# The four weight sums of each pair, made by adding DMAs in place of VectorE sums

## The chip, the cores and the metric

The kernel runs on one NeuronCore of a Trainium2 chip. The metric is device time in microseconds (us), the median of three executions. Engines in the views: PE is TensorE (PEld its weight loads), DVE is VectorE, ACT is ScalarE, POOL is GpSimd, SP is SyncE, which here only issues DMAs. A "q" after an engine's name (SPq, ACTq) is its instruction queue when it issues a DMA.

## What is computed

A decoder block over 1024 tokens of width 1024, in fp32: a pooling mixer and a sliding-window attention, merged by sigmoid gates, then a squared-ReLU MLP. The change touches two of its matrix products, the gates and the first MLP matrix:

```python
proj = jnp.einsum('bsd,de->bse', h, w_in[l]) + b_in[l]
u_pool, q, k, v, gates = jnp.split(proj, IN_SPLITS, axis=-1)      # gates: 2048 columns
...
g = jax.nn.sigmoid(gates.astype(jnp.float32)).astype(x.dtype)
...
ff = jnp.einsum('bsf,fd->bsd',
                jnp.square(jax.nn.relu(jnp.einsum('bsd,df->bsf', h2, w_up[l]))), w_down[l])
```

## The kernel before

Every fp32 operand of a matmul is split into a rounded part `hi` and a rest `lo`: `split` (L99 to L104) has ACT copy the source into `hi` (L101) and DVE subtract (L104). A block of 128x512 results then costs three matmul passes (`PASSES`) for each 128 of the contraction.

Gates and up both go through the class `Pairs`. It takes output rows of 128 in pairs and computes each pair by a 2x2 block scheme with seven products where the plain one has eight. Row 2p of the weights lies in a raw tile `r0` of 128x1024: its left half is A11, its right half A12. Row 2p+1 lies in `r1`: A21 and A22. There are 8 pairs for the gates and 16 for up. The seven products use these weight operands, by number:

- 1: A11; 2: A12; 4: A22 (no sum needed)
- 5: S1 = A21 + A22 (L492, into a tile `ws` of the pool `ga`)
- 6: S2 = S1 - A11 (L495); 7: S3 = A11 - A21 (L502); 3: S4 = A12 - S2 (L499)

`load` (L481) loads a raw tile from DRAM, `operand(p, i)` makes the sum and the split, `mm` (L515, matmuls at L519) runs the 12 matmuls of a product, `m1` and `m2` run products 1 and 2, and `rest` runs 6, 7, 5, 4 and 3 in this order, with DVE adding the results out of PSUM between them (L540 to L560). The other side of each product (`T1` to `T4`) are sums of blocks of the activations: `build_gate` makes them for the gates (from L722), `build_second` for up (from L1061). `gate_close0`, `gate_close1` and `up_close0`, `up_close1` apply sigmoid or relu and square, and store.

Gates: a first part runs products 1 and 2 of all pairs (`first`, `second`) in an order written out by hand for PE, DVE, ACT and SP; within it stand the operands 6 and 7 of pair 0 and `build_gate` for the blocks kt = 1, 2, 3. The loop after it runs `rest` for pairs 0 to 7. Up: a part with an order written out by hand for PE, DVE and ACT runs products 1 and 2 of pairs 0 to 6, builds the T tiles and makes pair 0's operands; then `rest(0)` and a loop over pairs 1 to 15, in which pairs from 7 on run their products 1 and 2 too. Outside the parts written by hand, a planner decides when the program is built in which order each engine takes its instructions: by when its own clock says that they are ready, and by program order among those. On the chip the order of each engine is fixed; an instruction whose data is late holds up all behind it on its engine.

Buffers: raw tiles come from `st` (3 slots) and, for the odd row of later pairs, from `g` (17 slots). Split operands 5, 6, 7 go to `ga` (6 slots) for the gates and `x1` (4 slots) for up, the others to `wh` (6 slots). Before the change POOL issues no DMA; the loads are issued by SP, stores by SP and ACT.

Of the kernel before, what the change touches and what calls it, by code (L numbers as in the profile page):

```python
# [8 lines left out]
F32 = mybir.dt.float32  # L9
# [41 lines left out]
def block_kernel(ctx: ExitStack, tc, xt, x, consts, vecs, sinks, b_qkv, g_post, g_mlp, g_mlp_post,  # L51
# [96 lines left out]
    vec = cp.tile([P, V_N], F32, name="vec")  # L148
# [68 lines left out]
    for k in range(NK):  # L217
        xs = at("s4", 4, [S])
        ws = stage([768]) if k else ws_first
        if k < 2:  # L220
            if k == 0:
                nc.sync.dma_start(vec, vecs)
            for a, b in ((0, 256), (256, 512)) if k == 0 else ((0, 512),):
                nc.sync.dma_start(xs[:, a:b], xt[k][:, a:b])
            if k:
                nc.sync.dma_start(ws, w_qkv[k])
            else:
                nc.sync.dma_start(ws[:, 512:], w_qkv[k][:, 512:])
            later.append((k, xs))
        else:  # L230
            nc.sync.dma_start(xs, xt[k])
            nc.sync.dma_start(ws, w_qkv[k])
            if k == 2:
                for i, t in later:
                    nc.sync.dma_start(t[:, 512:], xt[i][:, 512:])
# [32 lines left out]
    dve.tensor_scalar(nsnk, snk, -1.0, None, ALU.mult)  # L268

# [199 lines left out]

    OPERAND = {1: "B11", 2: "B21", 3: "B22", 4: "T4", 5: "T1", 6: "T2", 7: "T3"}  # L470

    class Pairs:


        def __init__(self, src, big, result, close_first, close0, close1):
            self.src, self.big, self.result = src, big, result
            self.close_first, self.close0, self.close1 = close_first, close0, close1
            self.X = {n: [None] * 4 for n in OPERAND.values()}
            self.raw, self.w, self.sums, self.f0, self.b1 = {}, {}, {}, {}, {}
# [6 lines left out]
        def operand(self, p, i):  # L486

            r0, r1_ = self.raw[2 * p], self.raw.get(2 * p + 1)
            if i in (5, 6, 3):
                if p not in self.sums:  # L490
                    self.sums[p] = ga_.tile([P, 2, 4, P], F32, tag="ga", name=nm("ws"))
                    dve.tensor_tensor(self.sums[p][:, 0], r1_[:, :4], r1_[:, 4:], ALU.add)  # L492
                src, s2 = self.sums[p][:, 0], self.sums[p][:, 1]
                if i == 6:
                    dve.tensor_tensor(s2, src, r0[:, :4], ALU.subtract)  # L495
                    src = s2
                elif i == 3:
                    src = r0[:, 4:]
                    dve.tensor_tensor(src, src, s2, ALU.subtract)  # L499
            elif i == 7:  # L500
                src = r0[:, :4]
                dve.tensor_tensor(src, r0[:, :4], r1_[:, :4], ALU.subtract)  # L502
            else:
                src = r0[:, :4] if i == 1 else r0[:, 4:] if i == 2 else r1_[:, 4:]
            t = self.big([2, 4, P]) if i in (5, 6, 7) and p else wslot([2, 4, P])
            split(t[:, 0], t[:, 1], src)
            self.w[p, i] = t
# [25 lines left out]
        def rest(self, p, f1, b6, b7, b5, done=(), then=None, b4=None):  # L533
# [4 lines left out]
            if 6 not in done:  # L538
                self.mm(b6, p, 6)
            dve.tensor_tensor(u2, u2, b6, ALU.add)  # L540
# [3 lines left out]
            if 7 not in done:  # L544
                self.mm(b7, p, 7)
# [151 lines left out]
    def gate_close(m, f):  # L697
        act.activation(f, f, AF.Sigmoid, bias=vec[:, V_BG + m:V_BG + m + 1])
        nc.scalar.dma_start(z_dram[m], f)
# [5 lines left out]
    def gate_close1(m, f):  # L705
        dve.tensor_tensor(f, f, rb, ALU.mult)
        gate_close(m, f)
# [14 lines left out]
    def build_gate(kt, place):  # L722

        ab = raw_x.pop(kt)
        act.activation(ab[0], ab[0], AF.Identity, scale=vec[:, V_G + kt:V_G + kt + 1])
        gb = vec[:, V_G + 4 + kt:V_G + 5 + kt]
        a0, a1, b0, b1 = (t[:, th * 512:(th + 1) * 512] for t in ab for th in range(2))
# [128 lines left out]
    with tc.manual_schedule(engines={mybir.EngineType.PE, mybir.EngineType.DVE, mybir.EngineType.Activation,  # L856
# [7 lines left out]
        for p in range(NG0):  # L864
# [39 lines left out]
    for p in range(8):  # L904
# [6 lines left out]
        for i in (6, 7, 5, 4, 3) if p else (5, 4, 3):  # L911
            gt.operand(p, i)
# [148 lines left out]
    def build_second(kt, b12, b22):  # L1061
# [4 lines left out]
        dve.tensor_tensor(r11, b12, r11, ALU.subtract)  # L1066
        dve.tensor_tensor(t2, b22, r11, ALU.subtract)
        dve.tensor_tensor(t3, b22, t3, ALU.subtract)
        dve.tensor_tensor(r21, r21, t2, ALU.subtract)
# [41 lines left out]
    def up_close1(m, f):  # L1111
        act.activation(f, f, AF.Relu)
# [66 lines left out]
    with tc.manual_schedule(engines={mybir.EngineType.PE, mybir.EngineType.DVE, mybir.EngineType.Activation}):  # L1179
# [25 lines left out]
        up.m2(2)  # L1205
        up.operand(0, 6)
        up.operand(0, 7)
# [338 lines left out]
```

## Time and profile before

| | us |
|---|---|
| median of 3 runs (lowest, highest) | 1115.41 (1114.57, 1115.86) |
| span of the profiled execution | 1112.6 |
| median less span | 2.8 |
| PE busy in the span | 1103.8 |
| DVE busy | 813.4 |
| ACT busy | 529.2 |
| POOL busy | 53.9 |
| gates: products 1 and 2 | 161.3 to 204.8 |
| gates: `rest`, pairs 0 to 7 | 204.8 to 313.9 |
| up: products 1 and 2 among transposes, pair 0 | about 480 to 547 |
| up: `rest`, pairs 1 to 15 | about 547 to 822 |
| second MLP matrix and end | 822 to 1112.6 |

The span runs from the first to the last instruction of the profiled execution; the time of a run has besides it what lies around the program. In the rows of the trace a group is given by line, engine, operation and "out<-in" with the shapes, then how often (x) and its busy time; in the timeline each row starts with its start and its length in us, and brackets tell how long the engine was idle before and what ended the wait.

### The profile page before, as it was taken

To read this page: it belongs to the slowest core of one execution; us is meant where nothing else is said; L and a number is where in the kernel's file an instruction comes from. 1 tells how busy PE (TensorE), PEld (TensorE's weight loads), DVE (VectorE), ACT (ScalarE), POOL (GpSimd) and SP (SyncE) were. 2 spreads that over 40 slices of the span, in tenths; PEclk is the share of its full clock that TensorE was granted. 3 is DMA by queue.
4 is the path that set the end of the run, shared out by engine and by line. 5 is a ranking of instruction groups with operands and counts; after the bars stand their busy time and mean duration, and the time that the engine had idled before them with its cause. 6 is when DMAs were issued, how large, how long until landed. Compare 5 with 4: busy or idle time off the path is not lost.

```text
span 1112.6 us, 13941 instructions
## 1 busy us (share of the span) xinstructions
PE 1103.8 (99%) x5162; PEld 916.6 (82%) x5162; DVE 813.4 (73%) x1217; ACT 529.2 (48%) x912; POOL 53.9 (5%) x104
## 2 busy tenths in 40 slices
PE   9999999999999999999999999999999999999997
PEld 8888888888888888888888888888888888888886
DVE  6578877898859966768978876766548945447797
ACT  7566656444323333636644544354444435344342
POOL 0334100000000500000000000000000000000000
PEclk9999999999999999999999999999999999999999
DMA  9615566366973543322356553434697766332652
GB/s 345 162 39 165 154 189 231 126 215 206 275 264 107 196 158 119 133 95 96 113 210 220 195 190 123 189 123 168 230 374 275 236 191 191 100 104 64 225 190 92
DMA packets 84435, 196.89 MB, mean 177 GB/s; under 512 B 7952, under 2 KB 20880, under 8 KB 84368
## 3 DMA queue, kind: packets, MB, share of 16 engines
q1 hardware_dynamic: 78608, 176.22, 47.1%
q10 hardware_dynamic: 5760, 19.79, 4.7%
q8 instruction: 40, 0.66, 0.2%
q14 instruction: 27, 0.22, 0.1%
HBM read 140.41 MB, written 55.58 MB: 176 GB/s over the span
## 4 chain that ended last, share of the span: by engine, by line
PE 96%; DVE 2%; ACT 1%; issue 0%; DVEq 0%; ACTq 0%
PE mm L519 25%; PE at L519 15%; PE at L1334 15%; PE mm L1334 12%; PE mm L1017 7%; PE mm L456 5%; PE mm L609 3%; PE mm L458 3%; PE mm L192 2%; PE mm L183 2%; PE sc L183 2%; PE sc L429 1%; PE sc L360 1%; PE at L1017 1%; PE at L1046 1%; PE sc L403 1%
## 5 line engine op out<-in xcount | busy, mean ns | idle before, releaser
L1334 PE MATMUL at<-ar,wh 128*128 128x512 f32 x696 | 158.7, 389 | 0.0
L1334 PEld LDWEIGHTS at<-ar,wh 128*128 128x128 f32 x696 | 130.6, 188 | 27.1
L1334 PE MATMUL mm<-ar,wh 128*128 128x512 f32 x576 | 131.0, 389 | 0.0
L1334 PEld LDWEIGHTS mm<-ar,wh 128*128 128x128 f32 x576 | 108.1, 188 | 22.5
L104 DVE TENSOR_TENSOR wh<-raw,wh 128x1024 fp32r<-128x1024 f32 x51 | 62.4, 1223 | 86.2 <-ACT wh L101 86.1
L101 ACT CAST wh<-raw 128x1024 fp32r<-128x1024 f32 x51 | 53.7, 1053 | 132.8 <-PE at L1334 53.8
L101 ACT CAST wh<-st 128x512 fp32r<-128x512 f32 (+1 forms) x104 | 65.6, 642 | 92.0 <-DVE st L499 25.8
L104 DVE TENSOR_TENSOR wh<-st,wh 128x512 fp32r<-128x512 f32 (+1 forms) x105 | 78.4, 756 | 37.3 <-ACT wh L101 34.7
L519 PE MATMUL mm<-gr,wh 128*128 128x512 f32 x333 | 79.3, 390 | 0.0
L519 PEld LDWEIGHTS mm<-gr,wh 128*128 128x128 f32 x333 | 62.2, 188 | 12.8
L519 PE MATMUL mm<-T,wx 128*128 128x512 f32 x288 | 67.4, 389 | 0.0
L519 PEld LDWEIGHTS mm<-T,wx 128*128 128x128 f32 x288 | 54.1, 188 | 11.2
L519 PE MATMUL at<-T,wx 128*128 128x512 f32 x252 | 58.9, 389 | 0.0
L519 PEld LDWEIGHTS at<-T,wx 128*128 128x128 f32 x252 | 47.3, 188 | 9.8
L519 PE MATMUL mm<-x,wh 128*128 128x512 f32 x240 | 55.2, 389 | 0.0
L519 PEld LDWEIGHTS mm<-x,wh 128*128 128x128 f32 x240 | 45.0, 188 | 9.4
L609 PE MATMUL mm<-x,wh 128*128 128x512 f32 x192 | 47.7, 395 | 0.0
L104 DVE TENSOR_TENSOR ar<-B,ar 128x1024 fp32r<-128x1024 f32 x37 | 45.1, 1220 | 2.3 <-ACT ar L101 2.0
L609 PEld LDWEIGHTS mm<-x,wh 128*128 128x128 f32 x192 | 35.2, 188 | 7.5 <-DVE qt L104 0.2
L101 ACT CAST ar<-B 128x1024 fp32r<-128x1024 f32 x37 | 38.9, 1051 | 4.7 <-DVE B L1305 2.8
L519 PE MATMUL at<-gr,wh 128*128 128x512 f32 x150 | 36.6, 390 | 0.0
L519 PE MATMUL mm<-T,wh 128*128 128x512 f32 x147 | 36.1, 389 | 0.0
(391 smaller groups left out, 2164.1 us busy)
## 6 DMA issues: line engine op xcount, KB each, us to landing
raw<-f_dram SPq DMA_DIRECT2D x53, 512.0 KB, 3.6
f_dram<-g SPq DMA_DIRECT2D x28, 512.0 KB, 3.3
st<-in_w_up_dram SPq DMA_DIRECT2D x24, 512.0 KB, 3.6
B<-in_w_dn_dram SPq DMA_DIRECT2D x24, 512.0 KB, 7.4
st<-in_w_g_dram SPq DMA_DIRECT2D x18, 512.0 KB, 4.2
f_dram<-g ACTq DMA_DIRECT2D x17, 512.0 KB, 3.1
g<-spill_dram SPq DMA_DIRECT2D x16, 512.0 KB, 5.0
raw<-in_w_dn_dram SPq DMA_DIRECT2D x16, 512.0 KB, 4.6
```

Source lines behind the costliest of these rows:

```text
L101: act.copy(hi, src)
L104: eng.tensor_tensor(lo, src, f32(hi), ALU.subtract)
L183: pe.matmul(bq, xs_[k][n // 4][:, xh, n % 4 * P:(n % 4 + 1) * P], wq[k][:, h, :], start=k == 0 and j == 0, stop=k == NK - 1 and j == 2)
L192: pe.matmul(bkv_of(n), xs_[k][n // 4][:, xh, n % 4 * P:(n % 4 + 1) * P], wkv[k // 2][:, h, k % 2, :], start=k == 0 and j == 0 and not (joi ...
L360: pe.matmul(sb[:, kv, i, :nk], qt[r, qx, m * P:(m + 1) * P], kx[r, k0:k0 + nk], start=j == 0, stop=j == 2)
L403: pe.transpose(bs[:, kv, m], s8[:, kv, m], ident)
L456: pe.matmul(bs[th], whi[:, k, :], rhs(k, hl, th), start=k == 0 and hl == 0, stop=False)
L458: pe.matmul(bs[th], wlo[:, k, :], rhs(k, 0, th), start=False, stop=k == nk - 1)
L519: pe.matmul(b, w[:, wh, kt, :], xo[kt][:, xh, :], start=not after and kt == 0 and j == 0, stop=kt == 3 and j == 2, skip_group_check=after)
L609: pe.matmul(b, (whi, wlo)[h][:, k, :], xr(k, xh, th), start=j == 0, stop=j == len(mms) - 1)
L1017: pe.matmul(obs[n][dj], l, wos[k][whl][:, dj * 512:(dj + 1) * 512], start=k == 0 and hl == 0 and whl == 0, stop=k == NK - 1 and hl == 1)
L1334: pe.matmul(bs[t], fo[fh][:, k2, t * P:(t + 1) * P], wo_[wh][:, k2, :], start=not after and s2 == 0 and k2 == 0 and j == 0, stop=(s2, k2) ...
```

## The change

The four sums of a pair are no longer made by DVE. GpSimd issues for each a DMA that adds a half row (128x512 fp32, 256 KB) from the weights in DRAM onto the half of a raw tile in SBUF. So that every sum is an addition, the second block row is taken with its sign turned: operand 7 is A11 + A21 (onto A11 in `r0`), operand 6 adds A22 to that, operand 3 adds A12 to that, and operand 5 is A21 + A22 (onto A21 in `r1`). Operands 7, 6 and 3 are so made one after the other in the same 128x512 of SBUF, each after the split of the one before has read it. The order in `rest` and in the calls of `operand` becomes 7, 6, 5, 4, 3. The turned signs are taken up by the T tiles (an addition for a subtraction, with the negated gain `neg_g` in `build_gate`), by one subtraction in `rest`, and by scale=-1 in `gate_close1` and `up_close1`. The tile `ws` goes away.

```diff
+    neg_g = vec[:, V_N:]
...
+    dve.tensor_scalar(neg_g, vec[:, V_G + 4:V_G + 8], -1.0, None, ALU.mult)
...
+    ADDEND = {7: (1, 0), 6: (1, 1), 3: (0, 1), 5: (1, 1)}
...
         def operand(self, p, i):
             r0, r1_ = self.raw[2 * p], self.raw.get(2 * p + 1)
-            if i in (5, 6, 3):
-                if p not in self.sums:
-                    self.sums[p] = ga_.tile([P, 2, 4, P], F32, tag="ga", name=nm("ws"))
-                    dve.tensor_tensor(self.sums[p][:, 0], r1_[:, :4], r1_[:, 4:], ALU.add)
-                src, s2 = self.sums[p][:, 0], self.sums[p][:, 1]
-                if i == 6:
-                    dve.tensor_tensor(s2, src, r0[:, :4], ALU.subtract)
-                    src = s2
-                elif i == 3:
-                    src = r0[:, 4:]
-                    dve.tensor_tensor(src, src, s2, ALU.subtract)
-            elif i == 7:
-                src = r0[:, :4]
-                dve.tensor_tensor(src, r0[:, :4], r1_[:, :4], ALU.subtract)
-            else:
-                src = r0[:, :4] if i == 1 else r0[:, 4:] if i == 2 else r1_[:, 4:]
+            src = r0[:, 4:] if i == 2 else r1_[:, 4:] if i == 4 else r1_[:, :4] if i == 5 else r0[:, :4]
+            if i in ADDEND:
+                row, half = ADDEND[i]
+                nc.gpsimd.dma_start(src, self.src[2 * p + row][:, 4 * half:4 * half + 4], accum_op=ALU.add)
             t = self.big([2, 4, P]) if i in (5, 6, 7) and p else wslot([2, 4, P])
             split(t[:, 0], t[:, 1], src)
...
         def rest(self, p, f1, b6, b7, b5, done=(), then=None, b4=None):
-            if 6 not in done:
-                self.mm(b6, p, 6)
-            dve.tensor_tensor(u2, u2, b6, ALU.add)
+            if 7 not in done:
+                self.mm(b7, p, 7)
             if p in self.b1:
                 self.f0[p] = f0
                 self.m2(p)
-            if 7 not in done:
-                self.mm(b7, p, 7)
+            if 6 not in done:
+                self.mm(b6, p, 6)
+            dve.tensor_tensor(u2, u2, b6, ALU.subtract)
...
-        gate_close(m, f)
+        gate_close(m, f, -1.0)
...
-        dve.tensor_tensor(a0, a1, a0, ALU.subtract)
+        dve.tensor_tensor(a0, a0, a1, ALU.subtract)
         dve.scalar_tensor_tensor(a1, b1, gb, a1, ALU.mult, ALU.subtract)
-        dve.scalar_tensor_tensor(b1, b1, gb, a0, ALU.mult, ALU.subtract)
-        dve.scalar_tensor_tensor(b0, b0, gb, b1, ALU.mult, ALU.subtract)
+        dve.scalar_tensor_tensor(b1, b1, gb, a0, ALU.mult, ALU.add)
+        dve.scalar_tensor_tensor(b0, b0, ngb, b1, ALU.mult, ALU.add)
...
             if p == 6:
-                gt.operand(0, 7)
+                gt.operand(0, 6)
...
             if p == 5:
-                gt.operand(0, 6)
+                gt.operand(0, 7)
...
-        for i in (6, 7, 5, 4, 3) if p else (5, 4, 3):
+        for i in (7, 6, 5, 4, 3) if p else (5, 4, 3):
...
-        act.activation(f, f, AF.Relu)
+        act.activation(f, f, AF.Relu, scale=-1.0)
...
+        up.operand(0, 7)
         up.operand(0, 6)
-        up.operand(0, 7)
...
-        for i in (6, 7, 5, 4, 3) if first else (1, 6, 2, 7, 5, 4, 3):
+        for i in (7, 6, 5, 4, 3) if first else (1, 7, 2, 6, 5, 4, 3):
```

`build_second` changes its four DVE sums in the same way.

More of the change, by code (lines that the diff above doesn't have):

```diff
@@ L147, in block_kernel @@
     cst = cp.tile([P, C_N], F32, name="cst")
-    vec = cp.tile([P, V_N], F32, name="vec")
+    vec = cp.tile([P, V_N + 4], F32, name="vec")
+    neg_g = vec[:, V_N:]
     snk = cp.tile([P, NH], F32, name="snk")
@@ L221, in block_kernel @@
             if k == 0:
-                nc.sync.dma_start(vec, vecs)
+                nc.sync.dma_start(vec[:, :V_N], vecs)
             for a, b in ((0, 256), (256, 512)) if k == 0 else ((0, 512),):
@@ L478, in __init__ @@
             self.X = {n: [None] * 4 for n in OPERAND.values()}
-            self.raw, self.w, self.sums, self.f0, self.b1 = {}, {}, {}, {}, {}
+            self.raw, self.w, self.f0, self.b1 = {}, {}, {}, {}
         def load(self, f, t=None):
@@ L695, in gate_first, with gate_close @@
         dve.tensor_tensor(f, b, rb[:, :512], ALU.mult)
-    def gate_close(m, f):
-        act.activation(f, f, AF.Sigmoid, bias=vec[:, V_BG + m:V_BG + m + 1])
+    def gate_close(m, f, sign=1.0):
+        act.activation(f, f, AF.Sigmoid, scale=sign, bias=vec[:, V_BG + m:V_BG + m + 1])
         nc.scalar.dma_start(z_dram[m], f)
@@ L726, in build_gate @@
         gb = vec[:, V_G + 4 + kt:V_G + 5 + kt]
+        ngb = neg_g[:, kt:kt + 1]
         a0, a1, b0, b1 = (t[:, th * 512:(th + 1) * 512] for t in ab for th in range(2))
-        dve.tensor_tensor(a0, a1, a0, ALU.subtract)
+        dve.tensor_tensor(a0, a0, a1, ALU.subtract)
         dve.scalar_tensor_tensor(a1, b1, gb, a1, ALU.mult, ALU.subtract)
-        dve.scalar_tensor_tensor(b1, b1, gb, a0, ALU.mult, ALU.subtract)
-        dve.scalar_tensor_tensor(b0, b0, gb, b1, ALU.mult, ALU.subtract)
+        dve.scalar_tensor_tensor(b1, b1, gb, a0, ALU.mult, ALU.add)
+        dve.scalar_tensor_tensor(b0, b0, ngb, b1, ALU.mult, ALU.add)
         yield
@@ L1065, in build_second @@
         act.copy(t3, b12)
-        dve.tensor_tensor(r11, b12, r11, ALU.subtract)
-        dve.tensor_tensor(t2, b22, r11, ALU.subtract)
+        dve.tensor_tensor(r11, r11, b12, ALU.subtract)
+        dve.tensor_tensor(t2, b22, r11, ALU.add)
         dve.tensor_tensor(t3, b22, t3, ALU.subtract)
-        dve.tensor_tensor(r21, r21, t2, ALU.subtract)
+        dve.tensor_tensor(r21, t2, r21, ALU.subtract)
         for name, src in (("T2", t2), ("T1", r11), ("T3", t3), ("B22", b22), ("T4", r21)):
```

## The prediction

> **What bounds the kernel now.** First the page: who is busy, and what the chain that ended last is made of.
>
> ```profile
> span 1112.6 us, 13941 instructions
> PE 1103.8 (99%) x5162; PEld 916.6 (82%) x5162; DVE 813.4 (73%) x1217; ACT 529.2 (48%) x912; POOL 53.9 (5%) x104
> PE 96%; DVE 2%; ACT 1%; issue 0%; DVEq 0%; ACTq 0%
> ```
>
> PE is the bound; at most 8.8 us of the span are not its work. The windows by stage tell where these lie (columns: stretch, its length, then busy us and instructions of PE, PEld, DVE, ACT, POOL, granted clock, DMA share, GB/s).
>
> ```profile
> 161.30:204.80 43.50, 43.50 (x193) 36.04 (x192) 33.83 (x52) 22.67 (x39) 0.00 (x0) 1.00 0.60 215
> 204.80:313.90 109.10, 109.06 (x481) 89.89 (x480) 93.45 (x137) 47.51 (x65) 0.00 (x0) 1.00 0.70 222
> 505.00:565.00 60.00, 60.00 (x278) 49.94 (x277) 51.87 (x85) 35.96 (x62) 0.00 (x0) 1.00 0.36 127
> 565.00:650.00 85.00, 85.00 (x376) 70.38 (x376) 69.75 (x112) 42.65 (x61) 0.00 (x0) 1.00 0.56 201
> 650.00:822.00 172.00, 172.00 (x760) 142.41 (x760) 108.15 (x161) 74.95 (x106) 0.00 (x0) 1.00 0.49 183
> 822.00:1112.60 290.60, 283.44 (x1257) 234.74 (x1255) 197.08 (x220) 123.76 (x157) 0.00 (x0) 1.00 0.53 176
> ```
>
> In every stage that the change touches PE is full to 0.04 us; 7.16 us of the 8.8 lie after 822, which it does not touch. Because a busy PE is modelled, I checked it by rate: `rest` of one gate pair is 60 matmuls, and the chain shows
>
> ```profile
> 218.94 13.60 PE mm L519 x60
> ```
>
> so 227 ns for each, and 481 of them are 109.0 us of the 109.10 of that stage: nothing is hidden between them. The waits of PE's weight loads give the only stall at a place that the change touches:
>
> ```profile
> PEld at L519 <- DVE gr L104: 0.5, 1, 0.5
> ```
>
> **What is removed.** The four sums of 24 pairs:
>
> ```profile
> L495 DVE TENSOR_TENSOR ws<-ws,st 128x512 f32<-128x512 f32 x24 | 16.6, 690 | 0.5
> L499 DVE TENSOR_TENSOR st<-st,ws 128x512 f32<-128x512 f32 x24 | 16.5, 687 | 0.2
> ```
>
> With the same count for L492 and L502, of the same shape, that is 96 x 0.69 = 66 us of DVE. They lie beside a full PE, so on the path they are worth nothing but the 0.5 us above. What they do give is room: DVE is busy 93.45 of 109.10 us in the gates' `rest`, and 8 x 4 x 0.69 = 22 us of these go.
>
> **What is changed at no cost.** The T tiles take as many DVE operations as before; the scale of an activation and the turned subtraction add no instruction. `neg_g` is one DVE operation on 128x4 in the prologue, like the row for `nsnk` (L268, 128x8):
>
> ```profile
> L268 DVE TENSOR_SCALAR nsnk<-snk 128x8 f32<-128x8 f32 x1 | 0.2, 165 | 0.0
> ```
>
> 0.2 us in a gap of DVE; without that cover still 0.2 us.
>
> **What is added.** 96 DMAs of 256 KB on POOL's queue, four for each pair, which POOL issues in order. POOL has nothing else to do in these stages (0.00 in the windows above). The trace of before has no adding DMA and no DMA issued by POOL, so its latency L, from the moment its last releaser is done to its landing, has to be bounded by plain ones (columns at the end: KB of each, median us to landing):
>
> ```profile
> out_dram<-st SPq DMA_DIRECT2D x8, 256.0 KB, 2.6
> st<-in_w_ba_dram SPq DMA_DIRECT2D x8, 256.0 KB, 5.0
> xr<-in_xt_dram SPq DMA_DIRECT2D x4, 512.0 KB, 10.1
> ```
>
> Below 2.6 us no row of this size goes, so no gain from that side; 10.1 us is the slowest load row of double the size, and an adding DMA moves as much, since it reads both summands. I take L = 5.0: same size, from DRAM to SBUF, beside the same traffic of the gates' stage, the row that it is nearest to. [...]
>
> **The new chain.** Operands 7, 6 and 3 are made in one place, so each DMA waits for the DVE half of the split before it. A split is a cast and a subtraction, of which the gates' opening shows both; the column after the start is the length:
>
> ```profile
> 201.52 0.69 DVE L492 TENSOR_TENSOR ws<-st 128x512 f32<-128x512 f32 x1
> 203.62 0.69 DVE L104 TENSOR_TENSOR wh<-ws,wh 128x512 fp32r<-128x512 f32 x1
> 205.54 0.62 ACT L101 CAST wh<-st 128x512 fp32r<-128x512 f32 x1 [1.96 <-DVE st L502]
> 206.19 0.69 DVE L104 TENSOR_TENSOR wh<-st,wh 128x512 fp32r<-128x512 f32 x1 [0.69 <-ACT wh L101]
> 206.80 2.49 DVE L104 TENSOR_TENSOR gr<-xr,gr 128x512 fp32r<-128x512 f32 x4
> 204.83 0.84 PE L519 MATMUL at<-T,wh 128*128 128x512 f32 x3
> ```
>
> A step is therefore L + 1.3 = 6.3 us, where a sum of 0.7 us stood. It matters at three places.
>
> (a) Opening of the gates' `rest`. DVE's order is written by hand: split of 7(0), then split of 6(0), then the four T splits of kt = 3 (206.80), which PE waits for. Now 7(0) can be split where L492 stood, until 202.2; the DMA of 6(0) lands at 207.2; cast and subtraction end at 208.5, and the T splits behind them on DVE start there, 1.7 us later than before. PE begins at 204.83 with 7(0) on three kt, 9 matmuls, to 206.9, and then waits for 6(0) until 208.5: 1.6 us, less the 0.5 that it waits now. Then the T splits end at 211.0, two gate results follow, and 5(0) is ready some 0.4 us after PE asks for it. Together +1.5 us. At L = 2.6 it is -0.5, at L = 10.1 about +6.6.
>
> (b) Opening of up, also by hand:
>
> ```profile
> 517.94 0.69 DVE L492 TENSOR_TENSOR ws<-st 128x512 f32<-128x512 f32 x1
> 521.94 0.58 ACT L526 COPY f<-mm 128x512 f32<-128x512 f32 x1
> 523.33 0.60 ACT L1080 ACTIVATE g<-mm 128x512 f32<-128x512 f32 x1 [0.80 <-PE mm L519]
> 523.82 1.13 ACT L101 CAST wh<-st 128x512 fp32r<-128x512 f32 x2
> 524.47 1.29 DVE L104 TENSOR_TENSOR wh<-st,wh 128x512 fp32r<-128x512 f32 x2 [1.70 <-ACT wh L101]
> 520.31 5.93 PE L519 MATMUL mm<-gr,wh 128*128 128x512 f32 x25
> ```
>
> 7(0) is split until 518.7, the DMA of 6(0) lands at 523.7, and ACT, held up by its cast, has behind it a copy, a relu and the casts of operands 1 and 2 of pair 6: the first of these is split at 526.7 in place of 525.1. PE does 24 matmuls of `m2(3)` and `m2(4)` from 520.31, to 525.75, and then wants it: 0.95 us late, of which the two matmuls on `hi` cover a little. +0.8 us. At 2.6 nothing, at 10.1 about +6.
>
> (c) The pairs that follow. If one pair's chain must end before the next begins, its period is three splits and two latencies, 3.9 + 2L = 13.9 us (the first DMA of a pair needs only the raw tile); if the next pair's operand 7 is split within it, 2(L + 1.3) = 12.6. PE takes 13.6 for a pair of the gates or of up's pairs 1 to 6, and 84 x 0.227 = 19.1 from pair 7 of up on. The lead that the operands have over PE decides what this costs:
>
> ```profile
> 214.01 0.68 DVE L495 TENSOR_TENSOR ws<-ws,st 128x512 f32<-128x512 f32 x1
> 218.78 0.84 PE L519 MATMUL mm<-T,ar 128*128 128x512 f32 x3
> 279.43 0.69 DVE L495 TENSOR_TENSOR ws<-ws,st 128x512 f32<-128x512 f32 x1
> 300.38 0.84 PE L519 MATMUL mm<-T,ar 128*128 128x512 f32 x3
> ```
>
> At gate pair 1 it is 4.8 us from the sum to PE, at pair 7 it is 21. So pair 1 has little cover: 6(1), one step after 7(1), which DVE reaches at about 216, is ready near 223.5, when PE (2 us late already) wants it: I add 0.8 us for pairs 1 and 2. From then on the lead holds at L = 5. A late cast also holds up ACT's closes and DVE's sums out of PSUM behind it; a pair takes three banks of four of its tag, and the same tag comes up again a pair later, so this has 13 us of cover, and the 2.75 us that DVE no longer spends in each pair pay for it.
>
> **The sum**: 0 + 1.5 + 0.8 + 0.8 = +3.1 us on a span of 1112.6, which is 1115.7. With the 2.8 us between the span and the median of 1115.41, the time is 1118.5.
>
> **Rivals.**
>
> *The chain becomes the bound* (slower by much). From L = 5.5 on even the overlapped period, 2(L + 1.3), passes 13.6, and each us more costs 2 us in each of 13 pairs (7 of the gates, 6 of up), less what lead there is. At L = 6, 1 us x 13 + 4 for the openings = +17: 1132; at 6.5 with some 4 us of lead, +27. For it: the 512 KB loads of the same weights are slower than this often enough,
>
> ```profile
> DMA to landing us min/median/max: 3.4/4.2/10.9
> ```
>
> and waiting casts stand in fixed queues. Against it: the median there is 4.2, and DVE has gained room.
>
> *Hidden altogether* (not slower). At L near 2.6 the adding DMA is done before DVE would have come through the sums: at (a) two or three sums in a row on DVE (201.52 to 205.5) go from ahead of the T splits, PE's 0.5 us wait vanishes, (b) and (c) cost nothing: 1112.1 + 2.8 = 1114.9. It decides for this below L = 3.4, where at (a) 6(0) is split as early as 206.9, as now. Faster by more than 0.5 us it can't be: there is no more idle time to win in these stages.
>
> *The DMAs crowd out others.* Where the attention outputs are loaded, the engines are full:
>
> ```profile
> 291.00:304.50 13.50, 13.50 (x62) 11.16 (x61) 10.09 (x13) 4.36 (x6) 0.00 (x0) 1.00 1.00 297
> ```
>
> Pair 7's four DMAs, 1 MB at 297 GB/s, push these loads by 3.5 us, 7 if both summands count. Their last split is at 304 and PE wants it at 313.9, so it takes 10 us to show: a price of 0 to 2 us, 1120 with the rest.
>
> *That the sums are not where they are wanted*, that is that the planner lays the DMAs out too late on POOL: then it looks like the first rival.
>
> **How the numbers follow.** Forecast with its small stalls 0.45 (1116 to 1122), chain as the bound 0.28 (1122 to 1145), hidden 0.20 (1114.6 to 1116), crowding 0.04, and 0.03 for a gain from a new order after 822, where the 7.16 us of idle time lie. The three runs of before lie within 0.12% of each other, so 0.2%, 2.2 us, is about what can be told from no change: up to 1117.6 is the same. A third of the forecast's own range is below that. So same 0.15 + 0.20 = 0.35, faster 0.04, slower 0.61. The range, 1114.8 to 1134, leaves out the upper half of the first rival and the little below.
>
> **What would show it.** Right: on POOL 96 DMAs with a median of 4 to 6 us to landing; PE waits of 1 to 2 us at the first product 6 of the gates and at `m1(6)` of up, named as waiting for L104 of `wh`; no PE wait in the loops after the first two pairs; DVE busy near 813.4 - 66 = 747. Wrong: PE waits in every pair of the gates' loop (chain as the bound), a median under 3.4 us with no PE wait (hidden), or a PE that does not wait while the time moves.

## The result and the profile after

The changed kernel takes 1231.21 us (median of four executions, 1229.83 to 1232.0), where the kernel before takes 1115.41: a ratio of 1.1039 with a 95% interval of 1.1023 to 1.1054, or 116 us more. The forecast was 1118.5 with a range to 1134. The profiled execution has a span of 1228.0 us, 115.4 more than before.

The busy line of the page of the changed kernel:

```profile
span 1228.0 us, 14193 instructions
PE 1142.4 (93%) x5162; PEld 934.6 (76%) x5162; DVE 753.0 (61%) x1122; ACT 529.3 (43%) x912; POOL 137.9 (11%) x200
```

DVE has lost 60 us of work, and PE, with the same 5162 matmuls, stands for 86 us instead of 9. Where it stands is seen by cutting both traces at the same matmuls: the gates' `rest`, the stages between, the first part of up (to its pair 1), up's pairs 1 to 15, and the remainder. (Up's pairs end at 800.6 us in the trace of before; the table ahead puts that end at 822, which changes no sum, since the 7.16 us of idle time of PE lie behind both.) Windows of before (stretch, its length, busy us and count of PE, PEld, DVE, ACT, POOL, granted clock, DMA share, GB/s):

```profile
204.80:314.00 109.20, 109.16 (x482) 89.95 (x481) 93.45 (x137) 47.61 (x65) 0.00 (x0) 1.00 0.70 223
314.00:491.90 177.90, 177.90 (x800) 146.57 (x799) 133.46 (x240) 70.76 (x141) 17.46 (x12) 1.00 0.43 151
491.90:547.60 55.70, 55.70 (x263) 46.45 (x262) 46.89 (x83) 34.96 (x69) 0.00 (x0) 1.00 0.26 95
547.60:800.60 253.00, 253.00 (x1118) 209.49 (x1117) 180.75 (x283) 119.45 (x171) 0.00 (x0) 1.00 0.49 180
800.60:1112.60 312.00, 304.84 (x1351) 252.48 (x1349) 207.44 (x231) 130.90 (x165) 0.00 (x0) 1.00 0.56 186
```

and of the changed kernel:

```profile
204.80:349.20 144.40, 118.53 (x481) 94.30 (x479) 75.35 (x106) 46.50 (x63) 24.45 (x28) 0.94 0.81 208
349.20:528.90 179.70, 178.28 (x799) 146.91 (x800) 134.21 (x242) 72.30 (x142) 17.47 (x12) 1.00 0.45 159
528.90:587.90 59.00, 57.13 (x263) 46.09 (x262) 39.70 (x71) 31.80 (x65) 8.73 (x10) 1.00 0.49 130
587.90:915.20 327.30, 280.37 (x1117) 223.12 (x1116) 147.57 (x231) 122.33 (x175) 47.20 (x54) 0.92 0.67 183
915.20:1228.00 312.80, 304.90 (x1351) 252.51 (x1349) 207.13 (x231) 131.02 (x165) 0.00 (x0) 0.99 0.56 186
```

The differences are 35.2 + 1.8 + 3.3 + 74.3 + 0.8 = 115.4 us: all but 6 lie inside the two loops over pairs. Each loop loses twice. PE stands (327.30 - 280.37 = 46.9 us in up, 25.9 in the gates), and its matmuls take longer while it runs: 280.37 us for 1117 of them against 253.00 for 1118, another 27.4 us in up and 9.4 in the gates, at a granted clock of 0.92 and 0.94.

What PE waited for (us in total, times, longest; `z` is a tile of the gates, `g` one of up):

```profile
PE at L510 <- DVE g L538: 22.9, 7, 5.0
PE mm L510 <- DVE g L538: 21.6, 7, 4.1
PE at L510 <- DVE z L538: 15.9, 3, 6.5
```

L538 is `v7 = u2 + b7`, DVE's sum out of the PSUM bank of product 7, and L536 is the sum ahead of it, which takes product 6 into `u2`. Product 4 is put on top of that bank, so it can't start before L538 has read it. Up's pairs show why that sum is late; the timeline at one of them (start, length, engine, line, operation; in brackets the idle time before it and what ended it):

```profile
828.91 5.60 PE L510 MATMUL at<-T,wx 128*128 128x512 f32 x24
829.27 0.62 ACT L101 CAST wx<-st 128x512 fp32r<-128x512 f32 x1 [4.05 <-DMA st<-in_w_up_dram]
829.92 0.69 DVE L104 TENSOR_TENSOR wx<-st,wx 128x512 fp32r<-128x512 f32 x1 [6.28 <-ACT wx L101]
...
831.02 0.89 POOL L495 DMA_DIRECT2D st<-in_w_up_dram  x1 [8.92 <-DVE wx L104]
835.05 0.62 ACT L101 CAST wx<-st 128x512 fp32r<-128x512 f32 x1 [4.15 <-DMA st<-in_w_up_dram]
835.70 0.69 DVE L104 TENSOR_TENSOR wx<-st,wx 128x512 fp32r<-128x512 f32 x1 [4.49 <-ACT wx L101]
836.31 0.68 DVE L536 TENSOR_TENSOR g<-g,at 128x512 f32<-128x512 f32 x1
...
837.51 0.68 DVE L538 TENSOR_TENSOR g<-g,at 128x512 f32<-128x512 f32 x1
...
838.25 5.49 PE L510 MATMUL at<-T,wh 128*128 128x512 f32 x12 [3.73 <-DVE g L538]
```

PE has product 6 of this pair (the first 12 of the 24 matmuls from 828.91) done at about 831.6. L536 could have used it at once and L538 a step later, well before PE asks for product 4 at 834.5. But in DVE's fixed order the split of the *next* pair's operand 6 stands ahead of them, and that split waits for ACT's cast, which waits 4.15 us for its adding DMA, which POOL could issue only after the split of operand 7 at 829.92, which had waited for a DMA itself. The DMA of a pair that is not wanted yet holds up the sum that is wanted now. The price here is 3.73 us of standing and 2.6 us more for the 12 matmuls behind it (5.49 us in place of the 2.88 of a product at full clock), together 6.3 us, which is what these pairs are longer by (25.3 us from one product 4 to the next on the mean of pairs 8 to 14, against 19.0 before).

The gates show the same form. At their pair 4 product 6 is done at about 281, but the split of pair 5's operand 3 stands ahead of both sums:

```profile
285.95 0.69 DVE L104 TENSOR_TENSOR wh<-st,wh 128x512 fp32r<-128x512 f32 x1 [2.13 <-ACT wh L101]
...
287.27 0.69 DVE L538 TENSOR_TENSOR z<-g,at 128x512 f32<-128x512 f32 x1
...
288.01 1.65 PE L510 MATMUL at<-T,wh 128*128 128x512 f32 x3 [4.23 <-DVE z L538]
```

DVE sits idle for 2.13 us in front of that split, though products 6 and 7 are done.

### The profile page after: what moved, and what is told of

It reads as the page before. It is cut to its first block, busy times and chain, and to the rows that moved or that the text cites. A ratio compares the mean times of both kernels' runs of the same rounds, so it can differ in the third digit from the quotient of the medians.

```text
span 1228.0 us, 14193 instructions
## 1 busy us (share of the span) xinstructions
PE 1142.4 (93%) x5162; PEld 934.6 (76%) x5162; DVE 753.0 (61%) x1122; ACT 529.3 (43%) x912; POOL 137.9 (11%) x200
## 3 DMA queue, kind: packets, MB, share of 16 engines
q1 hardware_dynamic: 78608, 176.22, 42.9%
q0 software_dynamic: 13824, 25.17, 12.6%
## 5 line engine op out<-in xcount | busy, mean ns | idle before, releaser
L101 ACT CAST wh<-st 128x512 fp32r<-128x512 f32 (+1 forms) x108 | 67.7, 642 | 129.8 <-DMA st<-in_w_up_dram 78.5
L101 ACT CAST wh<-raw 128x1024 fp32r<-128x1024 f32 x51 | 53.7, 1053 | 131.5 <-PE at L1326 54.3
L104 DVE TENSOR_TENSOR wx<-st,wx 128x512 fp32r<-128x512 f32 x30 | 20.7, 691 | 113.9 <-ACT wx L101 113.9
L495 POOL DMA_DIRECT2D st<-in_w_up_dram x49 | 42.7, 882 | 382.5 <-DVE wx L104 157.1
L510 PE MATMUL at<-T,wh 128*128 128x512 f32 x114 | 43.3, 539 | 39.7 <-DVE g L538 22.9
L510 PEld LDWEIGHTS mm<-gr,wh 128*128 128x128 f32 x333 | 62.1, 188 | 13.6 <-ACT g L517 0.8
L510 PE MATMUL mm<-T,wh 128*128 128x512 f32 x147 | 47.8, 479 | 25.7 <-DVE g L538 21.6
L510 PEld LDWEIGHTS at<-T,wh 128*128 128x128 f32 x114 | 29.2, 268 | 51.3 <-DVE g L538 25.9
L510 PEld LDWEIGHTS mm<-T,wh 128*128 128x128 f32 x147 | 33.8, 237 | 38.2 <-DVE g L538 24.6
L101 ACT CAST wx<-st 128x512 fp32r<-128x512 f32 x30 | 18.6, 619 | 93.6 <-DMA st<-in_w_up_dram 93.6
L510 PE MATMUL mm<-x,wh 128*128 128x512 f32 x240 | 55.5, 390 | 2.1 <-DVE z L542 2.1
```

Of the source, the lines that this page charges most:

```text
L101: act.copy(hi, src)
L104: eng.tensor_tensor(lo, src, f32(hi), ALU.subtract)
L495: nc.gpsimd.dma_start(src, self.src[2 * p + row][:, 4 * half:4 * half + 4], accum_op=ALU.add)
L510: pe.matmul(b, w[:, wh, kt, :], xo[kt][:, xh, :], start=not after and kt == 0 and j == 0, stop=kt == 3 and j == 2, skip_group_check=after)
```

## The experiments

For each kernel the lengths of the two loops, cut at the same matmuls as above, beside its time:

| kernel | what makes the sums | time us | gates us | up us |
|---|---|---|---|---|
| before | DVE | 1115.41 | 109.2 | 253.0 |
| after | 96 DMAs | 1231.21 | 144.4 | 327.3 |
| e1_signs | DVE, new order and signs | 1119.09 | 109.2 | 256.1 |
| e2_nochain | 7, 5 DMA; 6, 3 DVE | 1160.91 | 120.3 | 283.6 |
| e3_bank | 96 DMAs, product 4 has its own bank | 1239.79 | 148.8 | 329.6 |
| e4_hand | 96 DMAs, hand order | 1267.62 | 162.3 | 341.6 |
| e5_beside | DVE, 96 adding DMAs beside | 1315.62 | 201.5 | 254.8 |
| e6_gates | gates DMA, up DVE | 1158.68 | 144.9 | 254.6 |
| e7_five | only 5 by DMA | 1121.12 | 113.0 | 255.9 |
| e8_seven | only 7 by DMA | 1142.71 | 116.8 | 268.4 |
| e9_uphand | up DMA, second hand order | 1150.20 | 109.2 | 282.4 |
| e10_dvehand | DVE, second hand order in up | 1166.38 | 109.2 | 304.0 |
| e11_beside2 | DVE, 44 adding DMAs, all ahead of the loops | 1216.04 | 110.0 | 257.0 |
| e12_allhand | 96 DMAs, third hand order | 1194.16 | 141.8 | 291.5 |
| e13_uphand2 | up DMA, third hand order | 1159.03 | 109.2 | 290.6 |
| e14_dvehand2 | DVE, third hand order in up | 1168.83 | 109.2 | 304.0 |
| e15_late | 96 DMAs, each later | 1218.53 | 148.3 | 309.2 |
| e16_one_less | 87 DMAs, 7 by DVE in up's pairs 7 to 15 | 1205.69 | 144.3 | 302.8 |

In e4 and e10 four or five matmuls of the next stage, 1 to 2 us, run within up's loop and are counted in it. Line numbers move by a few lines from kernel to kernel; the sum called L538 above is L541, L542 or L546 below.

### Order and signs without the DMAs

```
-nc.gpsimd.dma_start(src, self.src[2 * p + row][:, 4 * half:4 * half + 4], accum_op=ALU.add)
+dve.tensor_tensor(src, src, (r0, r1_)[row][:, 4 * half:4 * half + 4], ALU.add)
```

> The changed kernel with the four sums made by VectorE again, in place in the raw tiles; order 7, 6, 5, 4, 3 and turned signs stay, GpSimd issues no DMA. Theory (the adding DMAs make the operands late; their splits stand in VectorE's fixed order ahead of the sums out of PSUM, and TensorE, which puts product 4 on top of product 7's bank, waits for these): within 0.5% of before, 1110 to 1121 us, no TensorE wait over 1 us in the two loops. Rival (the new order costs it: after product 6 VectorE has two sums to make within product 5): TensorE waits before product 4 stay in most pairs, 1150 to 1230 us.

1119.09 us, ratio 1.0033 (1.0023 to 1.0043). Turning the signs and swapping 7 and 6 costs 3.7 us, 3.1 of them in up's loop; 112 us come with the DMAs.

### Fewer DMAs in a row

Operands 7 and 5 by DMA, 6 and 3 by DVE (`if i in (7, 5)` ahead of the two lines above):

> The changed kernel with only the sums 7 and 5 made by adding DMAs (48 of 96), 6 and 3 by VectorE, so that no DMA waits for a split of 7 or 6. Theory (it is the chain of DMAs, each behind a split, that comes late): most of the loss goes, 1113 to 1140 us. Rival (what costs is the traffic or the issuing of the adding DMAs): half of them leave about half of the loss, 1165 to 1185 us.

1160.91 us, ratio 1.0407 (1.0373 to 1.0440): 70 us of the 112 are gone with half of the DMAs, but 42 remain. This is above what the theory said and just below the rival; it can't tell them apart. The next two say more, with 24 DMAs each (`if i in (5,)` and `if i in (7,)`):

> Only operand 5 by DMA (24 DMAs), 7, 6 and 3 by DVE. Operand 5's DMA waits for no split, only for the raw tiles, so no chain has its latency in it. Theory: 1118 to 1123. Rival (so much for each DMA, 24 x 1.17 us): 1145 to 1150.

> Only operand 7 by DMA (24 DMAs), 5, 6 and 3 by DVE. The same number of DMAs as in the run with operand 5 alone, but this one waits for the split of operand 1, and the sum of 6 and its split wait for it. Theory (one latency in the loop from a free operand slot to the split of 6, which stands in DVE's order ahead of the sums out of PSUM): as with 7 and 5 together, 1155 to 1166. Rival (so much for each DMA): 1145 to 1150, the same as with 5 alone; or, if all of that run's loss came from operand 5: 1118 to 1123.

Operand 5 alone: 1121.12 us, ratio 1.0048 (1.0032 to 1.0064), 2 us above e1. Operand 7 alone: 1142.71, ratio 1.0238 (1.0218 to 1.0257), 24 above e1. The same number of DMAs, and the one that others wait for costs ten times as much. Operand 5 came out within its theory. Operand 7 came out below both forecasts, the theory's 1155 and the rival's 1145, and 7 and 5 together cost 18 us more than 7 alone: what operand 5's DMA costs depends on what else is late. The trace of operand 7 alone shows PE at the same sum again:

```profile
PE at L513 <- DVE g L541: 8.9, 4, 3.8
```

### A bank of its own for product 4

```
-                b4=None if p else bank("mm"))
+                b4=bank(tag) if p else bank("mm"))
```

and the same in up:

> The changed kernel with a PSUM bank of its own for product 4 in every pair, so that product 4 need not wait until VectorE has read product 7; product 3 still goes on top of product 5's bank. Theory (TensorE waits for VectorE through the bank): the waits before product 4 go, and those left stand before product 3, which VectorE has one product more time to free; 1150 to 1200 us. Rival (the operands themselves come too late for TensorE): 1220 us or more, with waits before products 7, 6 or 3 for the splits (L104).

1239.79 us in a single execution, so without an interval. The time is the rival's, but its long waits are not for splits, as the rival had it: the wait only moves one sum on, to `f1h = v7 + b5`, which stands ahead of product 3:

```profile
PE at L510 <- DVE g L542: 29.0, 7, 5.8
PE mm L510 <- DVE g L542: 23.4, 6, 6.9
```

So the bank is where the delay reaches PE, not what makes it: the sums behind L538 are late too.

### The two loops apart

Only `w_g`'s sums by DMA, up's by DVE:

> Only the gates' 32 sums by DMA, up's 64 by DVE. Theory: the loss is made pair by pair in each loop, by a wait in that pair, so the gates' part of the trace comes back and up's part vanishes: 1119 + 35 = 1150 to 1160. Rival (the loss of up is only a delay handed on from the gates, by buffers that never recover): 1120 to 1130 or over 1180.

1158.68 us, ratio 1.0381 (1.0352 to 1.0411). The gates take 144.9 us, as in the changed kernel, and up 254.6, as without DMAs: up's loss is not handed on from the gates.

### The DMAs without anybody who waits for them

All sums by DVE, and 96 adding DMAs onto a spare tile; in the program 32 stand behind a small POOL copy of the gates' first split and 64 behind one of up's:

> All sums made by DVE as in e1 (1119), and beside them 96 adding DMAs of 256 KB on the same queue (32 from the gates' first pair on, 64 from up's first pair on) that add onto a tile which nothing reads. Theory (the lateness of the operands is what costs, not the transfers): within 3 us of e1, 1117 to 1122. Rival (the DMAs themselves cost: memory bandwidth, POOL's issue, the port to SBUF; 112 us over 96 is 1.17 us each): 1160 to 1231.

1315.62 us, ratio 1.178 (1.1743 to 1.1816), which by the time alone is the rival's side. But the DMAs did not wait for the splits: they start at 1.74 us, each is issued when the one before it on the same tile has landed, and the last at 537.58. In POOL's order they held up POOL's part of the attention (PE stood 43.2 and 42.1 us for it) and the small copy, until 410.40, for which ACT's next cast waited 88.05 us and, through it, PE 82.98. After that, pairs 2 to 5 of the gates run with these DMAs beside them; the window of the kernel before over the same 241 matmuls stands first:

```profile
232.38:286.78 54.40, 54.40 (x241) 45.05 (x240) 49.89 (x75) 23.59 (x32) 0.00 (x0) 1.00 0.67 214
418.72:473.13 54.41, 54.41 (x241) 45.06 (x240) 47.09 (x73) 23.19 (x34) 7.81 (x9) 1.00 0.83 233
```

Nine adding DMAs in 54.4 us, one in 6.0, where the changed kernel has 28 in the 144.4 us of its gates' loop, one in 5.2, and 54 in the 327.3 us of up's, one in 6.1. PE does not lose 0.1 us by them. Transfers at about that rate, which nobody waits for, cost these pairs nothing.

In e11 two such DMAs a pair stand in the program behind a POOL copy of a split of their pair:

```
+            if p and i in (7, 5):
+                pool.tensor_copy(pad[:, 1:2], f32(t[:, 1, 0, :1]))
+                row, half = ADDEND[i]
+                nc.gpsimd.dma_start(spare, self.src[2 * p + row][:, 4 * half:4 * half + 4], accum_op=ALU.add)
```

> All sums by DVE as in e1 (1119), and beside them in pairs 1 and later of both loops two adding DMAs of 256 KB a pair (44 in all), let go by the splits of operands 7 and 5 of the pair, onto a tile which nothing reads. Repeats the run in which POOL's queue held up other work, without that fault. Theory (not the transfers): 1118 to 1124. Rival (1.17 us for each DMA): 1165 to 1172.

1216.04 us, ratio 1.0899 (1.0881 to 1.0918), again on the rival's side by the time alone. What PE waited for, and the last of the 44 DMAs:

```profile
PE mm L320 <- POOL qkv L304: 42.8, 2, 40.5
PE sc L433 <- POOL dv L104: 37.6, 4, 11.7
```

```profile
249.65 0.86 POOL L504 DMA_DIRECT2D spare<-in_w_up_dram  x1 [3.50 <-DMA spare<-in_w_up_dram]
```

The fault is the same: the copies wait for the splits, but the DMAs do not wait for the copies. All 44 were issued between 1.74 and 249.65, one behind the other ahead of POOL's part of the attention, and the gates' loop begins at 301.6 instead of 205. Neither loop has an adding DMA beside it, so their 110.0 and 257.0 us (e1: 109.2 and 256.1) say nothing of the transfers, and this run does not bear on the question; the window of e5 does.

### Orders by hand

Three times the orders were written out, so that a split of a DMA's result stands behind the sums that are wanted sooner. The first one covered DVE and ACT in both loops:

> The changed kernel with all 96 adding DMAs, but in both loops an order for VectorE and ScalarE written by hand: the operands of pair p+1 are split between the products of pair p, each behind the sums out of PSUM that TensorE needs next; raw tiles are loaded a pair earlier. Theory (the latency of the chain fits into a pair's time, only the planner's order is wrong for it): 1114 to 1130 us, no TensorE wait over 1 us from the third pair of a loop on. Rival (three DMAs of some 4.5 us in a row are too long for a pair of 13.6 us in any order): 1160 us or more, with TensorE waits in every pair of 13.6 us.

1267.62 us, ratio 1.1343 (1.1310 to 1.1377). It missed, and its time is on the rival's side. In that order PE waits, among others, for the sum of product 5 (L547), for casts of operands and for the copy of `m1` (L517):

```profile
PE mm L510 <- DVE g L547: 11.3, 6, 3.4
PE mm L510 <- ACT wx L101: 11.2, 6, 3.8
PE mm L510 <- ACT g L517: 6.9, 4, 1.8
```

The second took up alone, put the split of operand 6 of pairs 7 and later into the pair that uses it, operand 3 always, and loaded the raw weights a pair earlier:

```
+        mine = {3: (3,)} if 0 < p < NF0 else {0: (6,), 3: (3,)} if p else {}
+        if q < NF0:
+            nxt = {1: (7,), 2: (5,), 3: (4,), 4: (6,)}
+        else:
+            nxt = {1: (7,), 2: (2, 5), 3: (4,)}
```

(the keys are places in `rest`: 0 its start, 1 before product 6, 2 after `v7`, 3 after `f1h`, 4 after the first close; `mine` are operands of the pair itself, `nxt` of the next.)

> Up's 64 sums by DMA, the gates' by DVE; in up the orders of DVE, ACT and PE are written by hand so that each DMA has at least a product or two between the split that lets it go and the split of what it makes, and that no such split stands ahead of a sum out of PSUM that is wanted sooner; the raw weights are loaded one pair earlier. Theory (latencies of 5 us that stand in the planner's order of DVE and ACT, one behind the other, and so in front of L538): up's 75 us go almost entirely, 1118 to 1130. Rivals: the transfers themselves or POOL's queue cost (then the order is no cure): 1180 to 1200, as up's part of the whole change; half and half: 1135 to 1165, where the theory would be only a part.

> Control for the run before: the same hand order and earlier loads in up, with all sums by DVE. Both: near e1 (1119), 1114 to 1125. If it is much above that, the hand order has a price of its own, which has to be taken off the other run.

1150.20 us with the DMAs, ratio 1.0311 (1.0281 to 1.0342), and 1166.38 without, ratio 1.0448 (1.0430 to 1.0465). Up takes 282.4 us where the planned order with the same 64 DMAs took 327.3; and with DVE's sums in their place the hand order takes 304.0. The raw weights come a pair earlier in both; what that alone does with the planned order was not run. The 1150 lies in the band "half and half", and the control is far above its own: writing the order by hand has a price, and in that order DMAs are the cheaper way to make the sums by some 21 us of up, where in the planned one they are dearer by 71. From 709.27 on, the window of the hand order with all four sums of each pair by DMA reads

```profile
709.27:805.00 95.73, 95.73 (x423) 78.91 (x422) 51.37 (x81) 43.71 (x66) 16.52 (x19) 1.00 0.73 198
```

95.73 us of 95.73, 19 adding DMAs, full clock: 423 matmuls at 226 ns, the rate of before. Pairs 9 to 14 take 19.0 to 19.8 us from one product 4 to the next, where the changed kernel's take 25, and where the same order with DVE's sums takes 21.4. What is left in that run is in the earlier pairs and in the last, 25.1 us; the dearest stall is at the step from pair 6 to pair 7:

```profile
644.16 0.62 ACT L101 CAST wx<-st 128x512 fp32r<-128x512 f32 x1 [7.28 <-DMA st<-in_w_up_dram]
...
644.81 0.69 DVE L104 TENSOR_TENSOR wx<-st,wx 128x512 fp32r<-128x512 f32 x1 [7.21 <-ACT wx L101]
...
646.13 0.69 DVE L546 TENSOR_TENSOR g<-g,at 128x512 f32<-128x512 f32 x1
...
646.87 3.35 PE L513 MATMUL at<-T,wh 128*128 128x512 f32 x7 [7.52 <-DVE g L546]
```

the same figure in pure form: a cast waits 7.28 us for its DMA, the split behind it 7.21, the sum behind that is late, PE stands for 7.52.

The third order moved that cast, put 6 ahead of 5, and wrote out POOL's and SP's orders too; for both loops, for up alone, and for up with DVE's sums:

> The changed kernel with all its 96 adding DMAs; only the orders of PE, DVE, ACT, POOL and SP in both loops are written by hand, so that no split of a DMA's result stands ahead of a sum out of PSUM that is wanted before the DMA can have landed, POOL's order is 7, 3 of the pair before, 6, 5, and the raw weights are loaded two pairs ahead. Theory (the lost time is latency in fixed orders): gates near 109 to 115 us, up near 256 to 268, the whole 1116 to 1135. Rival (the DMAs have a price that no order hides: bandwidth, POOL's issue, SBUF's port): 1200 to 1235. Between, 1150 to 1180: the order explains up's late pairs and something else the rest.

> As the run before, with the gates' sums by DVE in their planned order. Theory: what was left in the first hand order of up (26 us: operand 6's DMA behind operand 5's on POOL, and in the step from pair 6 to pair 7 the cast of 7 waiting 7.3 us for its DMA ahead of pair 6's sums) goes: up from 282 to 256 to 265 us, the whole 1118 to 1128. Rival (a rest that order does not cure): 1140 to 1150 as before.

> Control: the same hand order in up with every sum by DVE. If an order that suits DMA suits sums on DVE too: 1114 to 1125. If it doesn't (the first hand order with DVE's sums took 1166, because casts on ACT wait for sums that stand late on DVE): 1140 to 1170.

1194.16 us (ratio 1.0718, 1.0691 to 1.0745), 1159.03 (1.0401, 1.0386 to 1.0417) and 1168.83 (1.0487, 1.0467 to 1.0505). All three are above what the theory said; the first lies just below its rival's 1200, the second above its theory and its rival, the third within its alternative. For the whole change this order takes 37 us back, nearly all of it in up (291.5 for 327.3). The gates' pairs 1 to 5 get shorter (14.3 to 15.4 us from one product 4 to the next, before 13.6, in the changed kernel 15.5 to 21.2), but the end of the loop, where the attention outputs are loaded, gives that back with waits of 4.43 us (pair 7) and 11.18 us (the step to the next stage). In up the third order does worse than the second, 290.6 us against 282.4 with the gates' sums on DVE in both: the stall of 7.52 us is gone, and PE waits 5.28 and 3.86 us for casts in pairs 2 and 3 instead. And again the DMAs are the better choice in a hand order: 290.6 against 304.0 us in up.

### Longer and fewer latencies

Ahead of every adding DMA that waits for a split, POOL copies the split's result (0.75 to 0.87 us a copy on the mean, where the expectation took 1 to 1.5):

```
+                late = {6: 7, 3: 6, 7: 1}.get(i)
+                if (p, late) in self.w and (i != 7 or self.src is w_up and p > 6):
+                    pool.tensor_copy(spare, f32(self.w[p, late][:, 1]))
```

> The changed kernel; ahead of each adding DMA that waits for a split (3 and 6 everywhere, 7 from pair 7 of up on) POOL copies that split's result onto a tile which nothing reads, so the DMA starts one POOL copy of 128x512 later (about 1 to 1.5 us). The number of DMAs, their bytes and the planned order rules are unchanged. Theory (the loop of a pair from a free slot through two DMAs to the sums that PE's product 4 waits for sets the pair's period): pairs 7 to 14 of up go from 25.1 us to 25.1 + 2 x the copy = 27 to 28, the other pairs by 1 to 3 us each, the whole 1265 to 1300. Rival (a price for each DMA, whatever its time): 1228 to 1240.

1218.53 us, ratio 1.0900 (1.0865 to 1.0935): 13 us *faster* than the changed kernel, though each such DMA is issued a copy later behind its split. Both sides missed, and the theory missed in sign. Up's pairs 8 to 14 take 21.7 us on the mean instead of 25.3. The timeline at one of them:

```profile
780.41 0.62 ACT L101 CAST wx<-st 128x512 fp32r<-128x512 f32 x1 [2.60 <-DMA st<-in_w_up_dram]
...
781.06 0.69 DVE L104 TENSOR_TENSOR wx<-st,wx 128x512 fp32r<-128x512 f32 x1 [4.09 <-ACT wx L101]
781.67 0.68 DVE L540 TENSOR_TENSOR g<-g,at 128x512 f32<-128x512 f32 x1
782.39 0.69 DVE L542 TENSOR_TENSOR g<-g,at 128x512 f32<-128x512 f32 x1
...
783.13 3.02 PE L514 MATMUL at<-T,wh 128*128 128x512 f32 x12 [0.51 <-DVE g L542]
...
787.23 0.69 DVE L104 TENSOR_TENSOR wx<-st,wx 128x512 fp32r<-128x512 f32 x1 [1.02 <-ACT wx L101]
```

With the copies in it the planner laid the work out otherwise: one split that waits for a DMA, that of the next pair's 7 (781.06), stands ahead of the sums L540 and L542; the split of 6 (787.23) has come behind them, where it has the time of products 4 and 3. PE stands 0.51 us there instead of 3.73, and product 4 takes 3.02 us instead of 5.49.

In the last run 7 is made by DVE from pair 7 of up on, 9 DMAs fewer:

> The changed kernel, but in pairs 7 to 15 of up operand 7's sum is made by DVE: 9 DMAs of 96 fewer, and one DMA instead of two between the split of operand 1 and the split of operand 6. Theory (two latencies in the loop): these pairs from 25.1 to 20 to 21.5 us, the whole 1190 to 1202. Rival (a price for each DMA, 112 us over 96): 9 x 1.17 = 11 us less, 1218 to 1224.

1205.69 us, ratio 1.0801 (1.0775 to 1.0827), 25.5 less than the changed kernel: more than twice the rival's 11, short of the least that the theory gave, 29. These pairs take 22.2 us on the mean, where 20 to 21.5 were forecast.

## Why the prediction was wrong

**That PE bounds the kernel, and that DVE's 66 us are worth nothing on the path**, was right: DVE lost 60 us of its 813, and no stage got shorter for it. **"At no cost"** for signs and order was not: e1, which has these alone, is 3.7 us longer than before, and in up PE waits there for L538, up to 1.0 us at a time.

**The latency** was right in its median. The issues of the adding DMAs (count, KB, median us to landing):

```profile
st<-in_w_up_dram POOLq DMA_DIRECT2D x49, 256.0 KB, 4.2
st<-in_w_g_dram POOLq DMA_DIRECT2D x26, 256.0 KB, 4.8
g<-in_w_up_dram POOLq DMA_DIRECT2D x15, 256.0 KB, 5.3
g<-in_w_g_dram POOLq DMA_DIRECT2D x6, 256.0 KB, 5.7
```

L was taken as 5.0; single DMAs took 3.9 to 9.4. The floor of 2.6 us was misread, since the trace of before has a row of this size at 2.1 (`out_dram<-xf`), but nothing hung on it. That an adding DMA moves as much as a plain one of double the size was the author's estimate: the trace counts 256 KB for each, 25.17 MB in all, but their packets took 12.6% of the 16 engines' span, 0.50% for a MB, where the largest queue of plain DMAs took 42.9% for 176.22 MB, 0.24% for a MB.

**The gates' opening** was right in size, and in mechanism but for the instruction that waits. Operand 6(0) is split and the T splits start when the prediction said, at 208.42 for 208.5. But PE waits for the first of these T operands (L101 of `gr`) and not for 6(0): 2.37 us where it waited 0.5, so +1.9 for the +1.5 forecast.

```profile
202.54 0.88 POOL L495 DMA_DIRECT2D st<-in_w_g_dram  x1 [1.34 <-DVE wh L104]
207.16 0.62 ACT L101 CAST wh<-st 128x512 fp32r<-128x512 f32 x1 [1.43 <-DMA st<-in_w_g_dram]
208.42 2.49 DVE L104 TENSOR_TENSOR gr<-xr,gr 128x512 fp32r<-128x512 f32 x4
209.39 0.79 PE L510 MATMUL at<-gr,wh 128*128 128x512 f32 x1 [2.37 <-ACT gr L101]
```

**Up's opening** was forecast at 0.8 us, and the stretch before pair 1 grew by 3.3. The wait that it named, before `m1(6)`, did not come: PE runs through there. What came are waits of 0.2 to 0.9 us, 1.9 in all, 13 to 17 us later, for T tiles and an operand whose casts and splits were late by then.

**The step that failed is (c)**, in two places. It compared the period of a pair's chain, 2(L + 1.3), with the period of PE, and from pair 7 of up on it saw 12.6 to 13.9 us against 19.1 and charged nothing. The chain's length is not what those pairs pay for: they lost 6 us each at a latency that the comparison calls harmless. And it said that a late cast holds up the closes and DVE's sums behind it, but that "this has 13 us of cover", because a bank comes up again a pair later. That is true of a bank as a whole and false of product 4, which goes onto the bank of product 7 of the *same* pair as soon as product 5 is done: the cover is the 2.72 us of product 5, less the two sums of 0.68 that have to run first. A split that stands ahead of these sums and is 4 us late costs PE most of that each time. The term (c), 0.8 us, was in truth some 105: 35.2 + 74.3 of the two loops, less 1.9 of the gates' opening and the 3.1 that up's loop grows by in e1 without a DMA.

**The rival "the chain becomes the bound"** had the sign and saw the "waiting casts" in fixed queues, but priced it by the chain's period and so at 17 to 27 us. Its sign came, PE waits in six of the eight pairs of the gates' loop, but they are waits for DVE's sums and, but for the opening, for no operand. Adding latency made the loop shorter (e15), because the order changed; removing a DMA from it helped, though by less than the loop's arithmetic gave (e16). A period of latencies does not explain the loss; places in an order do.

**Shown**, then: the DMAs as transfers cost nothing where nobody waits for them (e5, pairs 2 to 5 of the gates, 54.41 us for 54.40), nor with all four sums of a pair made by them, from 709 us on in e9 (226 ns a matmul); the order and signs cost 3.7 us (e1); the gates' loss does not cause up's (e6, up in 254.6 us); operand 5's DMA, which waits for no split, is nearly free when it stands alone (e7, 2 us over e1), operand 7's, at the head of the chain, is not (e8, 24 us); and with the same DMAs, other orders bring up from 327 to 282 to 309 us (e9, e13, e15). **Open** is how much of the loss of the gates and of up's first pairs an order could cure: none that was tried kept 13.6 us a pair there, though the gates' waits have the same form; the hand orders had a price of their own of 48 us in up with DVE's sums (e10, e14); and whether an order exists that makes all 96 sums by DMA at 1116 us was not found. No version beat the kernel before.

## What to carry to other kernels

When work is moved from an engine to a DMA, do not stop at comparing the chain's period with the bound's; look at each engine's queue for the first instruction that waits for the DMA, and ask what stands behind it and when the bound engine wants that. A sum of 0.7 us made by the engine itself holds up what stands behind it by 0.7; a DMA in its place held it up by some 4 us here, in an order made for the former, and such waits reached the bound engine through a short tie, product 4's bank. A total that looks like contention can come from a quite different stage: cut every run at the same instructions before reading it, and see in the trace that what was to run beside a stage did run beside it.

## What was not expected of the hardware

PE lost a third of the 110 us not by standing but by running slowly after it stood. The window of the changed kernel behind the wait of 3.73 us:

```profile
838.00:844.00 6.00, 5.75 (x14) 4.50 (x15) 3.11 (x6) 0.85 (x2) 0.57 (x1) 0.50 0.62 97
```

The granted clock is 0.50, and 12 matmuls take 5.49 us. In shorter windows of that trace it reads 1.00 up to 837.0, when PE has stood for 2.5 us, 0.82 from there to 837.5, 0.50 from 837.5 to 844.1, which is 5.85 us after PE began to run again, and 0.95 from 844.1 to 844.5. PE's busy time in the two loops grew by 27.4 + 9.4 = 36.8 us, 3% of the span, because 14 of the 23 pairs had matmuls slowed behind a wait. The length of the wait alone did not tell which: in e9 a wait of 1.94 us was followed by slow matmuls and one of 2.06 was not.

```profile
586.84 7.39 PE L513 MATMUL mm<-T,wx 128*128 128x512 f32 x24 [1.94 <-ACT wx L101]
690.17 3.01 PE L513 MATMUL at<-T,wh 128*128 128x512 f32 x12 [2.06 <-DVE g L546]
```

At a granted clock of 1.00 24 matmuls take 5.60 us and 12 take 2.88. An adding DMA also holds POOL for 0.86 to 1.18 us while it is issued, and what stands behind it in POOL's order waits too: in e11, DMAs that each waited there for the one before delayed the gates by 96.6 us (301.6 for 205.0).
